# Small array tiles for the delta-rule walk of a four-mixer decoder step

## The chip, the cores and the metric

The kernel runs on one core of one Trainium2 chip. Its time is the device time of one execution in microseconds (us). Three executions of the kernel before took 2918.29, 2924.04 and 2924.26 us; the median is 2924.04 us. The engines are named as in the profile: PE (TensorE, matrix products), PEld (its weight loads), DVE (VectorE), ACT (ScalarE), POOL (GpSimd), SP (the queue that issues most transfers).

## The reference

Two layers, each `h = h + W_out @ concat(gate * mixer(RMSNorm(h)))` over 2048 prompt tokens, 16 meta tokens and 8 single decode tokens, width 1024, all float32. The four mixers (HGRN2, gated delta rule, SSD, retention) have 4 heads of 64 channels each and read columns of one input projection. The change is in the gated delta rule alone. Cut to what matters, one chunk of it is:

```python
def chunk_gated_delta(S, xs):
    q, k, v, g, beta = xs
    G = jnp.cumsum(g, axis=-1)
    m = jnp.where(strict, einsum('bhik,bhjk->bhij', k, k) * decay * beta[..., None], 0.0)
    rhs = concatenate([v * beta[..., None], k * (beta * exp(G))[..., None]], axis=-1)
    sol = triangular_solve(eye + m, rhs, lower=True, unit_diagonal=True)
    u = sol[..., :dv] - einsum('bhik,bhkv->bhiv', sol[..., dv:], S)
    qk = einsum('bhik,bhjk->bhij', q, k) * decay
    o = einsum('bhik,bhkv->bhiv', q * exp(G)[..., None], S) + einsum('bhij,bhjv->bhiv', qk, u)
    S_new = exp(g_last) * S + einsum('bhjk,bhjv->bhkv', k * exp(g_last - G)[..., None], u)
```

The outcome doesn't depend on the chunk length, and the kernel uses blocks of 32 tokens for this mixer.

## The kernel before

The tokens are cut into one short tile (t = 0: 32 prompt rows, of which 16 are meta tokens, and 8 decode rows) and 16 tiles of 128; two tiles make a dense block of 256 columns. A layer runs the SSD mixer (stage C), then the projections of the delta rule (stage B), then HGRN2 (A) and retention (D), then the output projection. The big projections multiply two-part float32r numbers in three products each (lines 473 to 475 and 483 to 485, tile `pd`). All smaller products go through the helper `mm` at line 235 in plain float32; the trace shows two PE records for each of these.

The recurrence of the delta rule, `walkB` (line 1207), is a generator. `hook` (line 145) runs its next part after each piece of dense work of stages B, A and D, so the walk's instructions lie between other matmuls on PE. A simulation-led scheduler sets the final order of instructions on each engine by when their operands would be ready. Each engine then works through its list in order.

For each tile of 128 tokens the walk does this.
- `loadB` (line 1119) issues the transfers: q, k, v (`X.qkv`) and the inverses (`X.tc`) into one buffer `bld`, the scores (`X.ma`) into `bma`. Both hold, for each token row, four heads of 32 columns: only the diagonal 32 x 32 blocks are stored.
- `keysB` (line 1138) makes the operands. POOL spreads the inverses to a matrix `tb` of 128 x 128 a head, zero outside its four diagonal blocks (line 1143). With it four products make the solved keys (`ke`, into `nq`, keys and queries of a block side by side), and four more the solved values `X.wi` (lines 1183 and 1184: `tb` against `vs`, 128 x 128 by 64 columns a head).
- `stepB` (line 1189) runs for each of the tile's four blocks. The state `SB` holds two heads a tile, block-diagonal: 128 rows (two heads of 64 channels) by 2 x 64. Two products (lines 1194 to 1196), one for each pair of heads, multiply keys and queries by the state into `X.wo`: 64 rows (32 of keys, 32 of queries) by 256 columns. DVE adds the keys' half to `wi` (line 1197), four products `kt` x `wi` make the update (line 1201; contraction over 32 rows), `next_state` (line 286) decays the state on ACT and adds the update on DVE in two halves of 64 partitions. ACT copies the queries' half to `X.oq` (line 1205).
- At the end of the tile (line 1261) four products of the scores with `wi` go into `X.wo`. For them POOL has spread the scores `X.ma` to `mb` (line 1243), 128 x 128 a head like `tb`.

Stages A and B also use parts of the array: scores of 64 rows by 32 or 64 columns (`sc<-aq,ak`, `sc<-bk`). `pair` (line 198) gives them a PSUM bank for each head half, with the note that row tiles of the array may not share a bank.

Of the kernel before, what the change touches and what calls it, by code (L numbers as in the profile page):

```python
# [92 lines left out]
def body(tc, ctx, a, o, nch, depth, blks, off):  # L93
# [39 lines left out]
    def later(f):  # L133
        """emit f after the next piece of work that is put off"""
        pend.append(f)
        while len(pend) > 1:
            pend.pop(0)()
# [7 lines left out]
    def hook(n=1):  # L145
        """the next parts of the walk that runs beside other work"""
        credit[0] += n
        while credit[0] >= 1:
            credit[0] -= 1
            if walk and next(walk[0], 0) == 0:  # L150
                walk.pop()

    @contextmanager
    def inorder(names):
        """what is emitted inside is issued after what was emitted before, on these engines"""
        seen, left = {}, set(names)
        for i in reversed(nc.cur_bb.bb.instructions):
            e = i.engine
            if e in left:
                seen[e] = i  # L160
                left.discard(e)
                if not left:
                    break
        with ExitStack() as st:
            for i in seen.values():
                st.enter_context(tc.issue_after(i))
            yield
# [31 lines left out]
    def pair():  # L199
        """a bank per head half: row tiles of the array may not share a bank"""  # L200
        return psc.tile([128, 2, 512], F32, tag="sc", name="sc")
# [43 lines left out]
    # ---------------------------------------------------------------- constants  # L245
# [15 lines left out]
    def fill():  # L261
        nc.sync.dma_start(cst, a["c_tab"])
        tri = w1([128, 128], "tri")
        nc.sync.dma_start(tri, a["c_retm"][:, 704:832])
        V.tensor_copy(l128r, tri)
        V.tensor_scalar(nbf, C("u32c"), -NEG, NEG, ALU.mult, ALU.add)
        V.tensor_copy(ibf, ident)
        tt(strict, C("u32c"), C("hm0"), ALU.subtract)
        for x in (*sbd, tb, mb, hones):
            G.memset(x, 0.0)  # L270
        G.memset(hones[0:64, 0:1], 1.0)
        G.memset(hones[64:128, 1:2], 1.0)

    # block-diagonal states (two heads a tile), in turns
# [4 lines left out]
    # full triangles (upper halves written), in turns; outside of their use: norm weights, retention's decay  # L279
# [6 lines left out]
    mb = cp.tile([128, 4, 128], F32, name="mb")  # L286

    def next_state(L, m, pu, decay):
        """S = decay * S + update, block-diagonal"""
        old = L.S[m]  # L290
        beside = m == "B"
        new = sbd[3 * beside + L.turn[beside] % (3 - beside)]
        L.turn[beside] += 1
        if old is not None:
            low = (bk if beside else w1)([128, 2, 2, 64], "low")
            for p in range(2):
                S.mul(low[:, p], old[:, p], decay(p))
        for hh in range(2):
            rr = slice(64 * hh, 64 * hh + 64)
            pv = pu[rr, 0:128].rearrange("k (p v) -> k p v", p=2)  # L300
            if old is None:
                V.tensor_copy(new[rr, :, hh], pv)
            else:
                tt(new[rr, :, hh], low[rr, :, hh], pv, ALU.add)  # L304
        L.S[m] = new
# [9 lines left out]
    # ---------------------------------------------------------------- helpers  # L315
# [4 lines left out]
    def power(dst, src, k=0):  # L320
        """src ** -0.5 (k=0) or 0.5 (k=1)"""
# [23 lines left out]
    def rms_scale(hx, R):  # L345
        """1 / rms of the rows"""
# [6 lines left out]
    # ---------------------------------------------------------------- per layer parameters  # L353
    def load_layer(l):
# [38 lines left out]
        # forget gate bounds: softmax of the logits over the depth axis, cumulative  # L393
# [34 lines left out]
    # ---------------------------------------------------------------- dense pieces  # L428
# [66 lines left out]
    def xprep(L, t, hx, keep=False):  # L495
        """normalised rows of a token tile -> channel-major, in two exact parts, to DRAM or to the block's tiles"""
# [32 lines left out]
    def rowtile(b, nm):  # L529
        """token-major rows of 256 columns by tile"""  # L530
# [6 lines left out]
    def small(L, b, raw):  # L537
        """decays and step sizes from the narrow columns of a block's tiles"""
# [31 lines left out]
        # cumulative sums: ssd over the chunk, gdn over blocks of 32  # L570
# [15 lines left out]
    def group_scale(osrc, R, groups, eps):  # L586
        """rows scaled by 1 / rms of each group, in SBUF; eps: number or [R, groups]"""
# [26 lines left out]
    def finish(t, mi, osrc, R, eps, w, z, b=None):  # L614
        """group norm of the mixer rows; returns what takes them to channel-major, gate z [128, 2, R], and to DRAM"""
# [27 lines left out]
    # decode: partitions hold (head half, key), free (sample, pair, value)  # L643
# [12 lines left out]
    def dec_bcast(rows8):  # L656
        """[8, 256] rows -> [128 (hh k), (b p), 64]"""
# [8 lines left out]
    def pb(x, cols=None):  # L666
        """[128, 2, 8] channel-major sample columns -> [128, 8, 2, 64] broadcast over values"""
# [8 lines left out]
    def dec_sum(src, lhs, m):  # L676
        """sum over the key partitions"""
# [18 lines left out]
    # ---------------------------------------------------------------- HGRN2  # L696
# [4 lines left out]
    def mixA(L, W, b):  # L701
# [26 lines left out]
        for c0, Lc, tl in groups:  # L728
# [7 lines left out]
            def scores(h, w):  # L736
                """products of keys at j and queries at j + w in steps of h"""
# [127 lines left out]
    # ---------------------------------------------------------------- short convolutions  # L865
    def conv(L, ws, b, wi, key, hasb, out):
        """out: 3 tiles [128, 2, BW] (pairs of channel tiles)"""
# [53 lines left out]
    def conv_samples(L, wi, key, hasb, src, dst):  # L921
        """the taps come from the stored rows"""
# [29 lines left out]
    # ---------------------------------------------------------------- gated delta  # L952
# [17 lines left out]
    def prepB(L, bs):  # L970
        """what the blocks need before the states: inverses of the unit triangles"""
# [4 lines left out]
        # sums of squares of q per token and head  # L976
# [30 lines left out]
        def factors(j0, j1):  # L1007
            """factors of tiles j0 .. j1 from the sums of squares of their keys"""
# [21 lines left out]
        def scv(x, n0, n):  # L1030
            """blocks n0 .. n0 + n as [(block, row), head, column]"""
            return x[:, n0:n0 + n].rearrange("h n j i -> (n j) h i")

        # decay within blocks of 32
# [13 lines left out]
        def scores(b, t, pv, start):  # L1048
            """pv [rows, x, y, p, i]: keys by keys, keys by queries"""
# [45 lines left out]
        # negated inverse of the unit triangular blocks above the diagonal: even rows of a block in one partition,  # L1095
        # odd rows in another, each beside the whole block as it was
# [23 lines left out]
    def loadB(L, P, i):  # L1120
        """what a tile keeps in DRAM: q, k, v, inverses, scores; gates"""
# [9 lines left out]
        # a group's first tile may have to wait for the inverses  # L1131
# [5 lines left out]

    def keysB(L, X):
        """a tile's operands for the walk over its blocks, in parts"""
        P, i, t, Lc = X.P, X.i, X.t, X.Lc  # L1140
        for bb in range(Lc // 32):
            r = slice(32 * bb, 32 * bb + 32)
            gtt(tb[r, :, r], X.tc[r], bcm(C("hm0")[r], 1, 4), ALU.subtract)
# [11 lines left out]
        # running decay of a block, broadcast over key channels  # L1155
# [8 lines left out]
        # keys and queries of a block side by side, in turns  # L1164
# [17 lines left out]
        for h in range(4):  # L1182
            mm(pn[0:Lc, 256 + 64 * h:320 + 64 * h], tb[0:Lc, h, 0:Lc], vs[0:Lc, h], False, True)
# [4 lines left out]
    def stepB(L, X, bb):  # L1188
        """one block of the walk"""
        r = slice(32 * bb, 32 * bb + 32)  # L1190
        SB, wt = L.S["B"], X.wi
        if SB is not None:
            b0, w0 = 64 * (bb // 2), 256 * (bb % 2)
            for p in range(2):
                mm(X.wo[b0:b0 + 64, w0 + 128 * p:w0 + 128 * p + 128], X.nq[:, p, 64 * bb:64 * bb + 64],
                   SB[:, p].rearrange("k x v -> k (x v)"), p == 0, True)
            tt(wt[r], wt[r], X.wo[r, w0:w0 + 256], ALU.add)
# [5 lines left out]
        if SB is not None:  # L1203
            o0 = 32 * (bb + 1 - 2 * (bb % 2))
            S.copy(X.oq[r], X.wo[o0:o0 + 32, w0:w0 + 256])

    def walkB(L):
        """the tiles in turn, in parts; a tile's operands are made during the one before"""
# [19 lines left out]
        while done < NT:  # L1228
# [12 lines left out]
            for bb in range(X.Lc // 32):  # L1241
                r = slice(32 * bb, 32 * bb + 32)
                gcopy(mb[r, :, r], X.ma[r])
            for bb in range(X.Lc // 32):
# [16 lines left out]
            for h in range(4):  # L1261
                mm(pi[0:X.Lc, 64 * h:64 * h + 64], mb[0:X.Lc, h, 0:X.Lc], X.wi[0:X.Lc, 64 * h:64 * h + 64], h == 0, True)
# [11 lines left out]
    def decB(L, ys, epsq):  # L1274
# [5 lines left out]
        # rows of v, keys scaled to unit length  # L1280
# [43 lines left out]
    # ---------------------------------------------------------------- SSD  # L1324
# [8 lines left out]
    def mixC(L, W, b):  # L1333
# [14 lines left out]
        def front(t):  # L1348
            """log decays of the tokens up to i, in two exact parts"""
# [88 lines left out]
    def post(L, t, osb, R):  # L1438
        """gated rows -> normalised channel-major"""
# [59 lines left out]
    # ---------------------------------------------------------------- retention  # L1499
# [3 lines left out]
    def mixD(L, W, b):  # L1503
        if b.first:
# [4 lines left out]
            # beside the triangles' use  # L1509
# [90 lines left out]
    # ---------------------------------------------------------------- output projection  # L1600
# [28 lines left out]
    # ---------------------------------------------------------------- program  # L1629
# [9 lines left out]
    def decode(L, left=False):  # L1639
        """the next part of the decode step"""  # L1640
# [113 lines left out]
def trace(nc, inputs):  # L1754
    """declares the arrays, traces the program; returns arrays by name"""
# [30 lines left out]
```

## Time and profile before

| | us |
|---|---|
| median of three executions | 2924.04 |
| profiled execution, span from first to last instruction | 2924.2 |
| PE busy | 2811.0 |
| PEld, DVE, POOL, ACT busy | 2631.0, 1694.9, 1045.4, 1010.7 |

The span of the profiled execution agrees with the median, so nothing has to be added around it. In the trace an array tile is given as rows*columns (128*64: 128 rows of contraction, 64 output partitions), then the operand as partitions x columns. A matmul record lasts longer than the time until the next one may start, since matmuls are pipelined; costs are therefore read from start to start.

### The profile page before, as it was taken

What the parts mean: (1) busy time and instruction counts of PE and PEld (TensorE: products, weight loads), DVE (VectorE), ACT (ScalarE), POOL (GpSimd) and SP (SyncE); (2) the same over time, 40 slices, a digit from 0 to 9 for tenths busy, and PEclk for the clock granted to TensorE, in tenths of its full rate; (3) what the DMA queues carried; (4) which work ended last, traced back from release to release, by engine and by line L of the source; (5) the groups of instructions that cost most, each with busy time, mean ns of one, the idle gap of its engine ahead of it and who ended that gap; (6) DMA issues with size and microseconds to landing.
All of it is one profiled execution on the core that took longest, in us unless ns stands there. A gap on an engine that the chain in (4) does not pass through costs nothing.

```text
span 2924.2 us, 76217 instructions
## 1 busy us (share of the span) xinstructions
PE 2811.0 (96%) x31196; PEld 2631.0 (90%) x31196; DVE 1694.9 (58%) x4822; ACT 1010.7 (35%) x2547; POOL 1045.4 (36%) x2000
## 2 busy tenths in 40 slices
PE   6989999999999999999999999899999999999998
PEld 6889898988888899999999999888988888999998
DVE  6777765646566745364456767565556657445433
ACT  5545522333333412232244454133333333222221
POOL 4453555665232211110033543745742222112000
PEclk9999999999999999999999999999999999999999
DMA  7243364462231432247762433645432222331433
GB/s 181 68 151 118 127 163 122 133 188 76 63 112 60 129 95 88 74 128 212 215 204 93 127 106 103 152 128 152 139 101 69 78 99 83 96 116 63 134 131 109
DMA packets 391332, 349.92 MB, mean 120 GB/s; under 512 B 144312, under 2 KB 361904, under 8 KB 380744
## 3 DMA queue, kind: packets, MB, share of 16 engines
q1 hardware_dynamic: 387464, 335.96, 37.5%
q0 software_dynamic: 3520, 9.09, 1.5%
q8 instruction: 247, 4.05, 0.6%
q14 instruction: 101, 0.83, 0.1%
HBM read 247.06 MB, written 98.10 MB: 118 GB/s over the span
## 4 chain that ended last, share of the span: by engine, by line
PE 84%; DVE 6%; DMA 4%; POOL 3%; ACT 2%; issue 2%; SPq 0%; POOLq 0%; ACTq 0%; DVEq 0%
PE pd L473 10%; PE pd L474 10%; PE pd L483 10%; PE pd L484 10%; PE pd L475 10%; PE pd L485 10%; PE tr L235 7%; PE sc L235 5%; PE wo L235 5%; PE o L235 3%; DMA wr<-in_w_in_dram 1%; PE tr L611 1%; PE tr L507 1%; DVE hx L502 1%; POOL bR L1110 1%
## 5 line engine op out<-in xcount | busy, mean ns | idle before, releaser
L473 PE MATMUL pd<-xh,wh 128*128 128x256 f32 (+1 forms) x2816 | 832.1, 296 | 12.6 <-DVE hB L901 3.3
L474 PE MATMUL pd<-xl,wh 128*128 128x256 f32 (+1 forms) x2816 | 817.9, 290 | 0.0
L475 PE MATMUL pd<-xh,wl 128*128 128x256 f32 (+1 forms) x2816 | 814.1, 289 | 0.0
L483 PE MATMUL pd<-wh,xh 128*128 128x256 f32 (+3 forms) x2448 | 702.0, 287 | 6.4 <-DVE sraw L1342 4.6
L484 PE MATMUL pd<-wl,xh 128*128 128x256 f32 (+3 forms) x2448 | 700.8, 286 | 2.5 <-POOL wl L450 2.5
L485 PE MATMUL pd<-wh,xl 128*128 128x256 f32 (+3 forms) x2448 | 698.0, 285 | 0.2
L473 PEld LDWEIGHTS pd<-xh,wh 128*128 128x128 f32 x2816 | 543.9, 193 | 37.2 <-issue 16.8
L474 PEld LDWEIGHTS pd<-xl,wh 128*128 128x128 f32 x2816 | 543.8, 193 | 9.1 <-issue 6.6
L475 PEld LDWEIGHTS pd<-xh,wl 128*128 128x128 f32 x2816 | 543.6, 193 | 4.1 <-issue 2.6
L483 PEld LDWEIGHTS pd<-wh,xh 128*128 128x128 f32 (+1 forms) x2448 | 455.7, 186 | 12.6 <-issue 5.4
L484 PEld LDWEIGHTS pd<-wl,xh 128*128 128x128 f32 (+1 forms) x2448 | 455.8, 186 | 9.0 <-issue 3.4
L485 PEld LDWEIGHTS pd<-wh,xl 128*128 128x128 f32 (+1 forms) x2448 | 455.7, 186 | 4.4 <-issue 2.1
L304 DVE TENSOR_TENSOR sbd<-low,tr 64x128 f32<-64x128 f32 x384 | 109.0, 284 | 131.8 <-PE tr L235 113.4
L600 POOL TENSOR_SCALAR fm<-fm 128x4 f32<-128x4 f32 (+3 forms) x102 | 23.7, 233 | 419.2 <-DVE fm L597 393.1
L1613 DVE TENSOR_TENSOR hx<-hx,pd 128x256 f32<-128x256 f32 (+1 forms) x136 | 57.1, 420 | 175.5 <-PE pd L485 175.2
L327 POOL TENSOR_TENSOR fm<-fm,expo 128x4 f32<-128x4 f32 (+3 forms) x136 | 129.3, 951 | 49.0 <-DVE fm L602 38.7
L331 POOL TENSOR_SCALAR rm<-rm 128x1 f32<-128x1 f32 (+1 forms) x51 | 13.7, 269 | 367.2 <-ACT junk L349 366.3
L520 ACT ACTIVATE th<-pd 128x256 f32<-128x256 f32 (+2 forms) x162 | 62.3, 384 | 231.8 <-PE pd L475 194.9
L235 PEld LDWEIGHTS sc<-aq,ak 64*32 64x32 f32 (+1 forms) x7008 | 97.0, 108 | 39.7 <-issue 16.9
L235 PE MATMUL sc<-aq,ak 64*32 64x32 f32 (+1 forms) x7008 | 129.1, 200 | 2.5 <-ACT sq L773 2.0
L1110 POOL TENSOR_TENSOR bR<-bR,bW 128x120 f32<-128x120 f32 (+14 forms) x300 | 119.6, 399 | 21.6
L1109 POOL TENSOR_TENSOR bW<-bU,bR 128x120 f32<-128x120 f32 (+14 forms) x300 | 112.6, 375 | 36.4 <-DMA bR<-bscr 15.4
(519 smaller groups left out, 4989.0 us busy)
## 6 DMA issues: line engine op xcount, KB each, us to landing
xh<-xh SPq DMA_DIRECT2D x56, 1024.0 KB
xl<-xl SPq DMA_DIRECT2D x56, 1024.0 KB
wr<-in_w_in_dram SPq DMA_DIRECT2D x64, 512.0 KB
hx<-in_x_prompt_dram SPq DMA_DIRECT2D x32, 512.0 KB
y<-y SPq DMA_DIRECT2D x128, 128.0 KB
yf<-y SPq DMA_DIRECT2D x32, 512.0 KB
bld<-qkv SPq DMA_DIRECT2D x32, 384.0 KB
xh<-xh SPq DMA_DIRECT2D x8, 1184.0 KB
```

Of the source, the lines that this page charges most:

```text
L235: T.matmul(out, l, r, start=start, stop=stop, skip_group_check=True)
L304: tt(new[rr, :, hh], low[rr, :, hh], pv, ALU.add)
L327: G.tensor_tensor(dst, src, e.broadcast_to(list(src.shape)), ALU.pow)
L473: T.matmul(ps, hi[:, d], b.xh[:, d, 0:b.n], start=(d == 0), stop=False)
L474: T.matmul(ps, hi[:, d], b.xl[:, d, 0:b.n], start=False, stop=False)
L475: T.matmul(ps, lo[:, d], b.xh[:, d, 0:b.n], start=False, stop=(d == 7))
L483: T.matmul(ps[0:R, 0:n], xh[:, d], hi, start=(d == 0), stop=False)
L484: T.matmul(ps[0:R, 0:n], xh[:, d], lo, start=False, stop=False)
L485: T.matmul(ps[0:R, 0:n], xl[:, d], hi, start=False, stop=(d == 7))
L520: act(th[0:R, 0:n], ps, AF.Tanh, scale=0.5)
L1109: f(wv, bcm(U_[0:2 * nu, j, j + 1:32], 1, m), bcl(R_[0:2 * nu, 0:m, j], 31 - j), ALU.mult)
L1110: f(R_[0:2 * nu, 0:m, j + 1:32], R_[0:2 * nu, 0:m, j + 1:32], wv, ALU.subtract)
```

## The change

The block-diagonal operands are no longer multiplied whole. The state product becomes one product for each head, 64 rows by 64 columns, on the array tile of its own head half. The two products with `tb` (values) and `mb` (scores) become one for each head and block, 32 x 32, by a new helper `blocks32`. Each reads the packed operand directly. `mb` and its copies go. `tb` stays for the product that makes `ke`; its subtraction is now done in place for the whole tile and then copied. In `X.wo` a block now has 128 columns, and the two head halves lie in the upper and lower 64 partitions; DVE's addition and ACT's copy of a block are each split in two by head half.

```diff
+    def blocks32(out, lhs, rhs, Lc, start):
+        for h in range(4):
+            for bb in range(Lc // 32):
+                r = slice(32 * bb, 32 * bb + 32)
+                mm(out(r, h), lhs[r, h], rhs[r, h], start and h == 0, True)
@@ keysB
+        gtt(X.tc[0:Lc], X.tc[0:Lc], bcm(C("hm0")[0:Lc], 1, 4), ALU.subtract)
         for bb in range(Lc // 32):
             r = slice(32 * bb, 32 * bb + 32)
-            gtt(tb[r, :, r], X.tc[r], bcm(C("hm0")[r], 1, 4), ALU.subtract)
+            gcopy(tb[r, :, r], X.tc[r])
...
-        for h in range(4):
-            mm(pn[0:Lc, 256 + 64 * h:320 + 64 * h], tb[0:Lc, h, 0:Lc], vs[0:Lc, h], False, True)
+        blocks32(lambda r, h: pn[r, 256 + 64 * h:320 + 64 * h], X.tc, vs, Lc, False)
@@ stepB
-            b0, w0 = 64 * (bb // 2), 256 * (bb % 2)
             for p in range(2):
-                mm(X.wo[b0:b0 + 64, w0 + 128 * p:w0 + 128 * p + 128], X.nq[:, p, 64 * bb:64 * bb + 64],
-                   SB[:, p].rearrange("k x v -> k (x v)"), p == 0, True)
-            tt(wt[r], wt[r], X.wo[r, w0:w0 + 256], ALU.add)
+                for hh in range(2):
+                    rr = slice(64 * hh, 64 * hh + 64)
+                    mm(X.wo[rr, 128 * bb + 64 * p:128 * bb + 64 * p + 64], X.nq[rr, p, 64 * bb:64 * bb + 64],
+                       SB[rr, p, hh], p == 0, True)
+            def part(hh, q):
+                r0 = 64 * hh + 32 * ((bb + q) % 2)
+                return X.wo[r0:r0 + 32, 128 * bb:128 * bb + 128].rearrange("t (p v) -> t p v", p=2)
+            w4 = wt.rearrange("t (p x v) -> t x p v", p=2, x=2)
+            for hh in range(2):
+                tt(w4[r, hh], w4[r, hh], part(hh, 0), ALU.add)
...
-            o0 = 32 * (bb + 1 - 2 * (bb % 2))
-            S.copy(X.oq[r], X.wo[o0:o0 + 32, w0:w0 + 256])
+            for hh in range(2):
+                S.copy(X.oq.rearrange("t (p x v) -> t x p v", p=2, x=2)[r, hh], part(hh, 1))
@@ walkB
-            for bb in range(X.Lc // 32):
-                r = slice(32 * bb, 32 * bb + 32)
-                gcopy(mb[r, :, r], X.ma[r])
...
-            for h in range(4):
-                mm(pi[0:X.Lc, 64 * h:64 * h + 64], mb[0:X.Lc, h, 0:X.Lc], X.wi[0:X.Lc, 64 * h:64 * h + 64], h == 0, True)
+            blocks32(lambda r, h: pi[r, 64 * h:64 * h + 64], X.ma, X.wi.rearrange("t (h v) -> t h v", h=4), X.Lc, True)
```

The scheduler also lays the rest out anew. On PE, one walk step in stage A of layer 0 (seventh full tile, second block; `wo<-sbd` is the state product, `pd` the dense work, `sc` HGRN2's scores) stands like this before:

```order
L484 MATMUL pd<-wl,xh 128x256
L485 MATMUL pd<-wh,xl 128x256
L235 MATMUL wo<-sbd_113,bnq 64x128 x2
L483 MATMUL pd<-wh,xh 128x256
L484 MATMUL pd<-wl,xh 128x256
```

and like this in the changed kernel (whose line numbers are one lower there):

```order
L235 MATMUL sc<-aq,ak 32x32 x20
L235 MATMUL wo<-sbd_113,bnq 64x64
L235 MATMUL sc<-aq,ak 32x32
L484 MATMUL pd<-wh,xl 128x256
L482 MATMUL pd<-wh,xh 128x256
L483 MATMUL pd<-wl,xh 128x256
L484 MATMUL pd<-wh,xl 128x256
L235 MATMUL wo<-sbd_113,bnq 64x64 x3
L482 MATMUL pd<-wh,xh 128x256
```

The four products of the step no longer stand together: the first, which needs only the first head half of the state, is put ahead of dense work, and three follow later. Over the whole program the state products of the 128 steps stand in 179 runs instead of 128, the 130 updates in 155 instead of 130, and the score products of the 34 tiles in 49 instead of 40.

On PE, between the sixth and seventh full tile (`wo<-bwi,mb` are the score products, `tr<-bvs,tb` the products with the inverses, `tr<-tb,bke` the solved keys, `tr<-bwi,bkt` the update), before:

```order
L235 MATMUL sc<-aq,ak 32x32 x14
L235 MATMUL tr<-bwi,bkt 64x64 x4
L235 MATMUL tr<-tb,bke 64x128 x4
L235 MATMUL sc<-aq,ak 32x32 x2
L235 MATMUL wo<-bwi,mb 128x64 x4
L235 MATMUL sc<-aq,ak 32x32 x11
L235 MATMUL tr<-bvs,tb 128x64 x4
L235 MATMUL sc<-aq,ak 32x32 x5
L483 MATMUL pd<-wh,xh 128x256
```

and in the changed kernel:

```order
L235 MATMUL sc<-aq,ak 32x32 x17
L235 MATMUL tr<-bwi,bkt 64x64
L235 MATMUL tr<-tb,bke 64x128 x3
L235 MATMUL tr<-bwi,bkt 64x64 x3
L235 MATMUL tr<-tb,bke 64x128
L235 MATMUL sc<-aq,ak 32x32 x6
L235 MATMUL wo<-bwi,bma 32x64 x16
L235 MATMUL sc<-aq,ak 32x32 x7
L235 MATMUL tr<-bvs,bld 32x64 x16
L235 MATMUL sc<-aq,ak 32x32 x2
L472 MATMUL pd<-xh,wh 128x256
```

Four products by head became sixteen by head and block at the same places, and the update and the solved keys are now cut into one and three. Counted over the whole order, two neighbouring matmul rows have different array tiles at 1195 places before and at 1376 in the changed kernel.

On POOL, at the same tile (`fm` are norm factors, `bgx` a broadcast of decays, `sq` HGRN2's triangles), before:

```order
L327 TENSOR_TENSOR fm<-fm,expo 128x4
L243 COPY bgx<-g 128x256
L243 COPY mb<-bma 32x4x32 x4
L1143 TENSOR_TENSOR tb<-bld,cst 32x4x32 x4
L327 TENSOR_TENSOR fm<-fm,expo 128x4
```

and in the changed kernel:

```order
L243 COPY tb<-bld 32x4x32 x4
L326 TENSOR_TENSOR fm<-fm,expo 128x4
L1147 TENSOR_TENSOR bld<-bld,cst 128x128
L243 COPY bgx<-g 128x256
L243 COPY sq_114<-aS 32x2x32 x8
```

The copies to `mb` are gone, and one subtraction on 128 partitions with four copies stands for four subtractions on 32.

## Rows read from the trace of the kernel before

**Rows 1.** The page's first part: span, engines' busy time, share, instructions.
```profile
span 2924.2 us, 76217 instructions
PE 2811.0 (96%) x31196; PEld 2631.0 (90%) x31196; DVE 1694.9 (58%) x4822; ACT 1010.7 (35%) x2547; POOL 1045.4 (36%) x2000
```
**Rows 2.** The page's chain that ended last, shares by engine.
```profile
PE 84%; DVE 6%; DMA 4%; POOL 3%; ACT 2%; issue 2%; SPq 0%; POOLq 0%; ACTq 0%; DVEq 0%
```
**Rows 3.** Waits of PE: us in total, times, longest.
```profile
PE tr L507 <- DVE hx L502: 13.2, 2, 10.4
PE tr L235 <- DVE bwi L1197: 12.3, 5, 5.3
PE tr L1146 <- DMA bld<-qkv: 11.7, 3, 6.5
```
**Rows 4.** PE groups: array tile, operand, records | busy, mean ns | idle before.
```profile
L235 PE MATMUL wo<-sbd,bnq 128*64 128x128 f32 x512 | 83.9, 287 | 0.5 <-DVE sbd L304 0.2
L235 PE MATMUL wo<-bwi,mb 128*128 128x64 f32 (+1 forms) x272 | 36.7, 274 | 0.0
L235 PE MATMUL tr<-bvs,tb 128*128 128x64 f32 (+1 forms) x272 | 34.9, 271 | 0.0
```
**Rows 5.** Timeline of PE, a state product between dense work: start us, us, what.
```profile
500.13 0.28 PE L474 MATMUL pd<-xl,wh 128*128 128x256 f32 x1
500.25 0.28 PE L475 MATMUL pd<-xh,wl 128*128 128x256 f32 x1
500.46 0.65 PE L235 MATMUL wo<-sbd,bnq 128*64 128x128 f32 x4
501.04 0.39 PE L473 MATMUL pd<-xh,wh 128*128 128x256 f32 x1
501.26 0.28 PE L474 MATMUL pd<-xl,wh 128*128 128x256 f32 x1
```
**Rows 6.** Timeline of PE, an update between dense work.
```profile
496.13 0.28 PE L473 MATMUL pd<-xh,wh 128*128 128x256 f32 x1
496.33 0.45 PE L235 MATMUL tr<-bwi,bkt 32*64 32x64 f32 x8
496.71 0.39 PE L474 MATMUL pd<-xl,wh 128*128 128x256 f32 x1
496.94 0.28 PE L475 MATMUL pd<-xh,wl 128*128 128x256 f32 x1
```
**Rows 7.** Timeline of PE, HGRN2's 64-wide scores around an update.
```profile
794.32 0.45 PE L235 MATMUL sc<-aq,ak 64*64 64x64 f32 x8
794.70 0.45 PE L235 MATMUL tr<-bwi,bkt 32*64 32x64 f32 x8
795.07 0.45 PE L235 MATMUL sc<-aq,ak 64*64 64x64 f32 x8
```
**Rows 8.** Timeline of PE, the products with the inverses between small scores.
```profile
721.42 1.10 PE L235 MATMUL tr<-bvs,tb 128*128 128x64 f32 x8
722.46 0.32 PE L235 MATMUL sc<-aq,ak 64*32 64x32 f32 x10
```
**Rows 9.** Timeline of PE, the score products of tile 0 (one block).
```profile
462.49 0.63 PE L235 MATMUL wo<-bwi,mb 32*32 32x64 f32 x8
463.05 1.02 PE L235 MATMUL tr<-dV,hones 128*2 128x512 f32 x2
```
**Rows 10.** Timeline of PE, a long run of small scores.
```profile
682.45 0.82 PE L235 MATMUL sc<-aq,ak 64*32 64x32 f32 x64
683.20 0.38 PE L474 MATMUL pd<-xl,wh 128*128 128x256 f32 x1
```
**Rows 11.** DVE and ACT groups by shape: as rows 4.
```profile
L1197 DVE TENSOR_TENSOR bwi<-bwi,wo 32x256 f32<-32x256 f32 x128 | 53.3, 416 | 82.9 <-PE wo L235 81.0 <-PE o L235 0.4
L1067 DVE TENSOR_TENSOR bma<-sc,bdc 32x128 f32<-32x128 f32 x2 | 0.6, 278 | 0.1
```
**Rows 12.** Waits of POOL, columns as rows 3.
```profile
POOL mb L243 <- PE wo L235: 151.7, 23, 12.7
```
**Rows 13.** Waits of SP, columns as rows 3.
```profile
SPq L1130 <- DVE bnq L1169: 83.6, 10, 12.1
```

More of the change, by code (lines that the diff above doesn't have):

```diff
@@ L268, in fill @@
         tt(strict, C("u32c"), C("hm0"), ALU.subtract)
-        for x in (*sbd, tb, mb, hones):
+        for x in (*sbd, tb, hones):
             G.memset(x, 0.0)
@@ L285, in body @@
     tb = cp.tile([128, 4, 128], F32, name="tb")
-    mb = cp.tile([128, 4, 128], F32, name="mb")
     def next_state(L, m, pu, decay):
```

## The prediction

> **What bounds the kernel now.** I read the page's first part, then the chain, the waits of PE and, for prices, the timeline of PE. The first part shows PE busy for 2811.0 of 2924.2 us, while DVE, ACT and POOL are far below [rows 1]. The chain that ended last is PE for 84% [rows 2]: the reader is to see that the span is one long queue of matmuls. PE's waits are short. The three longest together are 37.2 us, and of these only the second and third have to do with the walk (24.0 us) [rows 3]. So what changes the length of PE's list changes the time nearly one for one, and what changes DVE, ACT or POOL counts only where PE comes to wait for it.
>
> The groups that the change touches are 512 + 272 + 272 records of PE [rows 4]. Their busy figures overlap, as a record lasts longer than the distance to the next, so I price everything from start to start.
>
> **Prices.** Dense matmuls follow each other at 0.12 us (500.13 to 500.25) [rows 5]. A state product, four records of 128 columns in one array tile, takes 0.58 us until dense work starts again [rows 5]. An update, eight records of 64 columns, takes 0.38 [rows 6]; HGRN2's 64 x 64 scores, also eight of 64 columns, take 0.38 too [rows 7]. In both of these two array tiles work side by side (the update's are two column halves, the scores' two row halves), so eight records are four steps. Four steps of 128 columns against four of 64 differ by 0.20 us, so a step of 64 columns is 0.05, and 0.18 of the 0.38 is fixed. The fixed part is the price of changing the array's tile. Rows 6 give the same: from 496.13 to 496.94 are 0.81 us, less 0.24 for two dense distances and 0.20 for four steps leaves 0.37 for two changes. Rows 7, where small tiles follow small tiles, give 0.375 - 0.20, about 0.17. One array tile alone checks the step: tile 0's score products, eight records of 64 columns in a single 32 x 32 tile, take 0.56, which is 8 x 0.05 + 0.16 [rows 9]. I use 0.16 to 0.185 for a change, and 0.16 in the sum, since most of the added ones stand beside small groups.
>
> **The change part by part.**
>
> State products. 128 steps each exchange four records of 128 columns (0.58) for eight of 64 columns in two tiles, upper rows to upper partitions and lower to lower. The 64 x 64 scores are the nearest row: 0.38. That is -0.20 x 128 = -25.6 us. If the two tiles took turns it would be 8 x 0.05 + 0.18 = 0.58, a gain of nothing.
>
> Products by block. 32 tiles, two groups each, make 64 visits. Before, eight records on the full array take 1.04 us between small scores (721.42 to 722.46) [rows 8]: the same 64 columns cost twice as much there as in a small tile. After, a visit has 32 records: four array tiles on the diagonal, eight records each. No row shows four diagonal tiles. From below, if records only had to be issued, the long run of small scores gives 64 records in 0.75 us, so 32 cost 0.37 [rows 10], which lies under the tile's own eight steps; so the best case is 8 x 0.05 + 0.18 = 0.58. From above, if the tiles take turns, 32 x 0.05 + 0.18 = 1.78. I take 0.58, because two column tiles in one bank [rows 6] and two row tiles in two banks [rows 7] both run side by side, and diagonal tiles share neither rows nor output partitions. That is -0.46 x 64 = -29.4 us; the bounds are -29 and +47.
>
> Changes of tile. The order shows 181 more places where neighbouring rows differ in array tile. They come from steps that the scheduler now cuts (51 more runs of state products, 25 of updates, 9 of score products) and from visits that stood in full-array surroundings. 181 x 0.16 = +29.0 us (33.5 at 0.185).
>
> Other engines. DVE's addition becomes two of 32 x 128: 2 x 278 - 416 = +0.14 us a step [rows 11], ACT's copy grows likewise, +18 us at most over 128 steps if all of it were in PE's way. It isn't: PE waited for this addition in only 5 steps [rows 3], because a step's update follows its state product by several us of dense work (496.33 after the one before, 500.46 the next [rows 5, 6]). I cost it at nothing; without that cover it is 18 us. POOL loses the copies to `mb`, before which it sat idle for 151.7 us [rows 12], which frees whatever stood behind them; no wait of PE's three longest ends there, so nothing too. The buffer `bld` is now held until the products with the inverses, later than its last reader before (`bnq`), for which SP already waits 10 times [rows 13]. PE waited for that load in 3 tiles [rows 3]; if each of these waited another 7 us, roughly the distance of two steps, it is 21 us. I take nothing, as the load is issued a tile ahead.
>
> Sum: -25.6 - 29.4 + 29.0 = -26.0. From the profiled span of 2924.2, which is the median of the runs within 0.2, that is 2898 us.
>
> **A rule against it.** What the trace shows is side-by-side work for row tiles only with a bank for each [rows 7], and the kernel's own `pair` is written for that. The Trainium skill, TensorEngine Tiling (Array Packing), Restrictions and Gotchas, says that different row tiles cannot access the same PSUM bank at once. The changed kernel does let them: four row tiles write one bank of `pn` or `wo`, each to its own partitions. No run here shows whether distinct partitions lift the rule; by it the sum would be that of the first rival, by the rows it stays.
>
> **Rivals.**
>
> First, slower: row tiles that write one bank take turns. Place: the 64 visits and the 128 state products. Price: (1.78 - 1.04) x 64 = +47.4, state products 0, changes +29.0, together +76, so 3000 us (2985 to 3025). For it speaks `pair`'s note and that no row shows the case; against it that column tiles do share a bank [rows 6]. It decides below two tiles at a time: with two, a visit is 16 x 0.05 + 0.18 = 0.98, which gains 4 us in all.
>
> Second, no change: exactly that case, two at a time in the 32 x 32 groups. -25.6 - 4 + 29 = -0.6, so 2924.
>
> Third, the work shrinks and PE waits instead: the longer step on DVE and ACT (up to 18) and the later release of `bld` (up to 21) come out, with the split steps making each half of a state product wait for its half of the state. 2898 + 39 = 2937 at worst, about 2918 if half comes. For it: 24.0 us of such waits exist now [rows 3]. Against: they come in 8 places out of 128 steps.
>
> **How the numbers follow.** Forecast 0.60, with its own range 2882 to 2914 (the price of a change, some waits more or fewer). First rival 0.16, second 0.10, third 0.14. A measurement of this kernel can tell 0.2% (6 us) from no change. Faster by more than that is the forecast and a third of the third rival: 0.64. Within: the second and about a third of the third, 0.14. Slower: the first, and the rest, 0.22. The range 2880 to 2955 holds forecast, second and third; it leaves out the first (0.16) and a little below.
>
> **What would show it.** PE's records should rise by 2 x (2 x 32 x 12 + 128 x 2) = 2048 to about 33244. A run of 8 state records should take 0.38 to the next start, a visit of 32 records 0.55 to 0.65; 1.8 says the first rival, 1.0 the second. Updates in two runs with 0.16 to 0.18 lost at each edge confirm the third term. PE's waits for `bwi` and `bld` well above 24 us would be the third rival. The prediction is wrong if the visits come out at the size of rows 8 or more, or if PE's waits grow by more than the 26 us saved.

## The result, and the profile after

The changed kernel takes 2889.51 us (median of 4 executions, 2883.72 to 2890.53), against 2924.15 us of the kernel before beside it: a ratio of 0.9885, 95% interval 0.9865 to 0.9906. That is 34.6 us less; 26 were forecast. The profiled execution went from a span of 2924.2 to 2887.0 us, 37.2 us less.

The first part of the profile's page, which answers to [rows 1], and its chain by engine, which answers to [rows 2]:

```profile
span 2887.0 us, 80538 instructions
PE 2788.1 (97%) x33244; PEld 2605.7 (90%) x33244; DVE 1717.3 (59%) x4950; ACT 1030.2 (36%) x2675; POOL 997.6 (35%) x1903
...
PE 82%; DVE 6%; POOL 3%; DMA 3%; ACT 2%; issue 2%; SPq 1%; POOLq 0%; ACTq 0%; DVEq 0%
```

PE has the 2048 more records that were counted, and is busy for 22.9 us less. It still bounds the kernel. The waits of PE, in us, times and longest, as [rows 3]:

```profile
PE tr L506 <- DVE hx L501: 13.0, 2, 10.3
PE sc L235 <- POOL cgu L1364: 10.7, 6, 4.4
...
PE pd L472 <- ACT bk L896: 5.6, 4, 1.7
PE tr L235 <- POOL tb L243: 5.1, 1, 5.1
...
PE tr L235 <- DVE bwi L1212: 1.7, 2, 1.3
PE tr L1153 <- DMA bld<-qkv: 1.7, 1, 1.7
```

The two waits that had to do with the walk (`bwi` 12.3 and `bld` 11.7 us before) are down to 1.7 each, where the third rival had them grow.

The products with the inverses between dense work, on PE's timeline (start us, us, what); [rows 8] showed them before, between small scores:

```profile
475.88 0.28 PE L474 MATMUL pd<-xh,wl 128*128 128x256 f32 x1
476.09 0.65 PE L235 MATMUL tr<-bvs,bld 32*32 32x64 f32 x32
476.67 0.39 PE L472 MATMUL pd<-xh,wh 128*128 128x256 f32 x1
476.89 0.28 PE L473 MATMUL pd<-xl,wh 128*128 128x256 f32 x1
```

32 records take 0.58 us from start to start, as forecast: four diagonal tiles that write one bank work side by side. Within the visit the trace starts four records within 0.02 us, and each next four 0.06 to 0.08 us later. A state product in one piece, which answers to [rows 5]:

```profile
479.48 0.28 PE L474 MATMUL pd<-xh,wl 128*128 128x256 f32 x1
479.69 0.45 PE L235 MATMUL wo<-sbd,bnq 64*64 64x64 f32 x8
480.07 0.39 PE L472 MATMUL pd<-xh,wh 128*128 128x256 f32 x1
480.29 0.28 PE L473 MATMUL pd<-xl,wh 128*128 128x256 f32 x1
```

0.38 us, again as forecast. And one that the scheduler has cut:

```profile
837.23 0.28 PE L474 MATMUL pd<-xh,wl 128*128 128x256 f32 x1
837.44 0.33 PE L235 MATMUL wo<-sbd,bnq 64*64 64x64 f32 x2
837.69 0.39 PE L472 MATMUL pd<-xh,wh 128*128 128x256 f32 x1
837.92 0.28 PE L473 MATMUL pd<-xl,wh 128*128 128x256 f32 x1
838.13 0.44 PE L235 MATMUL wo<-sbd,bnq 64*64 64x64 f32 x6
838.50 0.39 PE L474 MATMUL pd<-xh,wl 128*128 128x256 f32 x1
838.72 0.28 PE L472 MATMUL pd<-xh,wh 128*128 128x256 f32 x1
```

The single product takes 0.25 us and the other three 0.37, together 0.62 for 0.38 in one piece. The reader is to see why: alone in its tile, the first product's two records have nobody beside them, and of the three others one tile has four records and the other two. Six steps stand for four, besides the second entry and exit. The whole price of the cut is read from dense record to dense record: 837.23 to 838.72 are 1.49 us, less four dense distances of 0.12 leaves 1.01; in one piece 479.48 to 480.29 are 0.81, less two leaves 0.57. So this cut costs 0.44 us.

**Where the time went, by a count over the trace.** For every pair of neighbouring PE records I took the distance of their starts and subtracted the median distance of the same pair (tile, columns, operands, with or without a change just before) in all traces of this study. An excess over 0.3 us counts as a wait; the excess of over 20 ns at records in stretches whose granted clock is half (1.2 GHz) counts as clock; the rest is PE's work. Each column is from one profiled execution; the ends of the span (about 18 us) are left out. Cuts are runs of state products above 128, plus runs of updates above 130; changes are places in PE's order where the array tile differs, all relative to the kernel before.

| kernel | median us | ratio and 95% interval | changes | cuts | span | work | waits | clock |
|---|---|---|---|---|---|---|---|---|
| before | 2924.15 | | 0 | 0 | 2924.2 | 2785.0 | 86.6 | 34.3 |
| changed | 2889.51 | 0.9885 (0.9865 to 0.9906) | +181 | 76 | 2887.0 | 2763.1 | 73.3 | 32.4 |
| e1 state products only | 2925.59 | 1.0027 (1.0015 to 1.0039) | +114 | 68 | 2922.9 | 2784.8 | 85.6 | 34.7 |
| e2 products by block only | 2886.68 | 0.9888 (0.9870 to 0.9905) | +25 | 0 | 2895.1 | 2758.2 | 84.5 | 34.6 |
| e3 tile by tile | 2940.80 | 1.0076 (1.0058 to 1.0093) | +169 | 81 | 2940.6 | 2809.0 | 77.0 | 36.7 |
| e4 late half first | 2885.10 | 0.9879 (0.9858 to 0.9900) | +70 | 16 | 2871.4 | 2738.0 | 85.7 | 29.4 |
| e5 changed, longer step | 2922.35 | 1.0007 (0.9993 to 1.0022) | +111 | 49 | 2921.7 | 2751.0 | 92.0 | 59.5 |
| e6 as e1, late half first | 2901.02 | 0.9939 (0.9919 to 0.9960) | -10 | 8 | 2901.7 | 2760.4 | 81.5 | 41.4 |
| e7 as e4, own buffer | 2881.10 | 0.9866 (0.9850 to 0.9883) | +58 | 13 | 2879.8 | 2735.4 | 94.1 | 32.2 |
| e8 before, split adds | 2906.89 | 0.9964 (0.9951 to 0.9978) | +18 | 1 | 2904.3 | 2791.6 | 74.8 | 19.7 |
| e9 before, longer step | 2918.18 | 0.9994 (0.9982 to 1.0005) | -42 | 2 | 2915.7 | 2785.3 | 79.4 | 32.8 |
| e10 changed again | 2887.61 | 0.9880 (0.9859 to 0.9901) | +181 | 76 | 2886.5 | 2762.6 | 74.5 | 31.0 |
| e11 as e7, again | 2878.55 | 0.9856 (0.9837 to 0.9875) | +58 | 13 | 2876.0 | 2735.3 | 94.3 | 28.0 |
| e12 as e2, split adds | 2900.56 | 0.9947 (0.9928 to 0.9966) | +18 | 1 | 2895.3 | 2758.9 | 88.9 | 29.4 |

Of the 37.2 us, 21.9 are less work of PE, 13.3 are shorter waits, 1.9 are clock. The line between work and waits hangs on how the pairs are formed: by shape alone, or by all operand names, the work of the changed kernel comes out 17 to 28 us less and its waits 18 to 7 us less, while the clock stays within 1 to 2. So differences of up to some 5 us in these two columns prove nothing.

### The profile page after: what moved, and what is told of

It is laid out like the page before. It is cut to its first block, busy times and chain, and to the rows that moved or that the text cites. A ratio compares the mean times of both kernels' runs of the same rounds, so it can differ in the third digit from the quotient of the medians.

```text
span 2887.0 us, 80538 instructions
## 1 busy us (share of the span) xinstructions
PE 2788.1 (97%) x33244; PEld 2605.7 (90%) x33244; DVE 1717.3 (59%) x4950; ACT 1030.2 (36%) x2675; POOL 997.6 (35%) x1903
## 4 chain that ended last, share of the span: by engine, by line
PE 82%; DVE 6%; POOL 3%; DMA 3%; ACT 2%; issue 2%; SPq 1%; POOLq 0%; ACTq 0%; DVEq 0%
PE pd L482 10%; PE pd L483 10%; PE pd L484 10%; PE pd L472 10%; PE pd L474 10%; PE pd L473 9%; PE tr L235 7%; PE sc L235 5%; PE wo L235 4%; PE o L235 3%; PE tr L610 1%; PE tr L506 1%; POOL bW L1108 1%; DMA wr<-in_w_in_dram 1%; POOL bR L1109 1%
## 5 line engine op out<-in xcount | busy, mean ns | idle before, releaser
L472 PEld LDWEIGHTS pd<-xh,wh 128*128 128x128 f32 x2816 | 541.1, 192 | 41.9 <-issue 12.1
```

The costliest lines, as they stand in the source:

```text
L472: T.matmul(ps, hi[:, d], b.xh[:, d, 0:b.n], start=(d == 0), stop=False)
```

## The experiments

Ratios are to the kernel before, run beside each group on the same chip (2916.37 to 2919.64 us there).

**Which half of the change carries it: e1 and e2.** e1 takes the changed kernel and puts `tb` and `mb` back for values and scores:

```diff
-        blocks32(lambda r, h: pn[r, 256 + 64 * h:320 + 64 * h], X.tc, vs, Lc, False)
+        for h in range(4):
+            mm(pn[0:Lc, 256 + 64 * h:320 + 64 * h], tb[0:Lc, h, 0:Lc], vs[0:Lc, h], False, True)
```

> State products on 64 x 64 tiles as in the changed kernel; the products by block back on the full array with tb and mb. Theory (time is the work of PE plus the changes of array tile): state products -25.6 us, and the order has 114 more changes than before at 0.16 = +18, so 2924 - 7 = 2917 us (2908 to 2922). Rival (the gain came from POOL no longer waiting to fill mb, and from PE's shorter waits): this keeps mb, so 2924 or a little more, and the products by block would carry all of the 34 us.

Measured: 2925.59 us, slower by 0.27% (0.15 to 0.39), outside the theory's range and at the rival's number. The work of PE is 2784.8 against 2785.0 us: nothing is left of 25.6, where 7 were to be left.

e2 takes the changed kernel and puts the state product, its addition and its copy back:

```diff
-                    mm(X.wo[rr, 128 * bb + 64 * p:128 * bb + 64 * p + 64], X.nq[rr, p, 64 * bb:64 * bb + 64],
-                       SB[rr, p, hh], p == 0, True)
+                mm(X.wo[b0:b0 + 64, w0 + 128 * p:w0 + 128 * p + 128], X.nq[:, p, 64 * bb:64 * bb + 64],
+                   SB[:, p].rearrange("k x v -> k (x v)"), p == 0, True)
```

> Products by block on 32 x 32 tiles as in the changed kernel; state products back on 128 x 64. Theory: -29.4 us for 64 visits, 25 more changes of tile than before at 0.16 = +4, so 2924 - 25 = 2899 us (2890 to 2906), visits of 0.58 us in the trace. Rival (POOL's share): about 2890, the changed kernel's whole gain without the state products.

Measured: 2886.68 us, as fast as the whole change and below the theory's range. Its work is 26.8 us less, where 25.4 were expected; the median fell by some 33, so the number is at the rival's, but the waits of its trace (84.5) are near those of before, and the work is there. Its profiled execution was its slowest (2896.83) and had a granted clock of 0.984, the other four 0.987 to 0.990; part of their gain is not in the trace. By their times alone e1 and e2 both speak for the rival. Against it speaks e6 below, which keeps `mb` and its copies and is still 18 us faster than the kernel before.

**Whether four tiles work side by side by themselves: e3.** The loops of `blocks32` are exchanged.

```diff
-        for h in range(4):
-            for bb in range(Lc // 32):
+        for bb in range(Lc // 32):
+            for h in range(4):
```

> The changed kernel with the loops of blocks32 exchanged: all four heads of one 32 x 32 tile follow each other, then the next tile. Same products. Theory (a tile works beside another only if PE's queue has reached the other's products, and it holds back behind one busy tile): a visit goes from 0.58 towards 32 x 0.05 + 0.18 = 1.78 us, 64 x 1.2 = up to +75 us, 2930 to 2965. Rival (the queue looks ahead over all 32 records): a visit stays at 0.58 to 0.65, 2890 to 2895.

Measured: 2940.80 us, slower than before. The timeline of PE in e3:

```profile
472.77 0.28 PE L474 MATMUL pd<-xh,wl 128*128 128x256 f32 x1
472.98 1.39 PE L235 MATMUL tr<-bvs,bld 32*32 32x64 f32 x32
474.30 0.39 PE L472 MATMUL pd<-xh,wh 128*128 128x256 f32 x1
```

The same 32 records take 1.32 us instead of 0.58, and 0.74 x 64 = 47 us is what the work column shows (2809.0 - 2763.1 = 45.9). The same products on the same tiles gain or lose by the order in which they are issued. In this visit the first five records start one by one, 0.05 to 0.08 us apart, and only from there on do some lie side by side.

**What a cut costs: e4 and e6.** The head halves are taken in the order 1, 0, so that a step's first product needs the half of the state that is written last, and all four become ready together.

```diff
-                for hh in range(2):
+                for hh in (1, 0):
                     rr = slice(64 * hh, 64 * hh + 64)
...
-        for h in range(4):
+        for h in (1, 0, 3, 2):
```

> The changed kernel with the head halves of the state product and of the update in the order 1, 0: the first product of a step needs the half that is written last, so the scheduler keeps the four together (144 runs of state products for 179, 130 of updates for 155, 111 fewer changes of tile in the order). Theory (a change costs 0.16 us of PE): 2889 - 18 = 2872 us (2866 to 2879). Rival (the changes are free, since PE waits a little anyway, or the early first product saves as much in waits): 2886 to 2893.

Measured: 2885.10 us, between the two ranges, and no clear difference from the changed kernel's 0.9885. The work fell by 25.1 us more than in the changed kernel, more than the 18 expected, but the waits rose by 12.4. Its executions range from 2873.14 us (the profiled one, clock 0.985) to 2891.74 (the other four have 0.981 to 0.984), so at the median more came back than the trace shows.

e6 makes the same edit in e1:

> State products alone on 64 x 64 tiles as in e1, but with the head halves in the order 1, 0 in state product and update, so that the four products of a step stay together (136 runs instead of 170, updates 130 instead of 156, 10 fewer changes of tile than in the kernel before). Theory (the state products' own gain of 0.20 us a step is real and e1 lost it to cut groups: two more changes and two more steps of a single tile for each cut): 2919.5 - 26 = 2894 us (2888 to 2901). Rival (64 x 64 tiles save nothing in this program, whatever the order): 2916 to 2926, as e1.

Measured: 2901.02 us, ratio 0.9939, clearly faster than e1. Work fell by 24.6 us (26.4 by the sum). So the state products' own gain is real when a step stays in one piece, and e1 lost it to its 68 cuts. 7 us of clock took part of it back.

**Whether the longer step is covered: e5 and e9.** Between state product and update, the block's values are multiplied by 1.0.

```diff
             for hh in range(2):
                 tt(w4[r, hh], w4[r, hh], part(hh, 0), ALU.add)
+            V.tensor_scalar(wt[r], wt[r], 1.0, None, ALU.mult)
```

> The changed kernel with one more DVE operation in every step: after the two additions the block's 32 x 256 values are multiplied by 1.0 in place, between state product and update. The order has 70 fewer changes of array tile, since the update now waits for one writer and is no longer cut (130 runs instead of 155). Theory (PE's list sets the time, a step's DVE work is covered, and 25 cuts fewer save 0.3 to 0.4 us each): 2878 to 2888 us. Rival (the walk's chain of DVE and ACT is in PE's way): at least 0.2 us more in each of 128 steps, 2889 + 25 = 2915 or more.

Measured: 2922.35 us, the rival's number: 33 us more than the changed kernel. Its work is 12.1 us less, as the fewer cuts and changes say, but waits are 18.7 and clock 27.1 us more. The largest wait of PE in e5 is for the added operation itself (line 1213); in the changed kernel PE waited 1.7 us for the block's values:

```profile
PE tr L235 <- DVE bwi L1213: 14.5, 11, 3.1
```

The mean granted clock of the changed kernel and of e5:

```profile
core 0: 2887.0 us, clock 0.985
```
```profile
core 0: 2921.7 us, clock 0.974
```

and PE in e5 at one place, where PE sat idle for 0.85 us and shortly before for 1.69 us, and then by stretches (start and end, length, busy time and instructions of PE, PEld, DVE, ACT and POOL, granted clock, DMA share and GB/s), first over 30 us and then in parts:

```profile
693.34 0.54 PE L235 MATMUL sc<-aq,ak 64*32 64x32 f32 x38 [1.69 <-issue]
...
699.01 0.68 PE L235 MATMUL sc<-aq,ak 64*64 64x64 f32 x16 [0.85 <-ACT sq L772]
699.87 0.45 PE L235 MATMUL tr<-bwi,bkt 32*64 32x64 f32 x8 [0.18 <-DVE bwi L1213]
```
```profile
690.00:720.00 30.00, 27.28 (x402) 24.37 (x400) 15.14 (x50) 9.49 (x30) 12.22 (x39) 0.72 0.30 74
...
691.00:693.50 2.50, 0.81 (x55) 0.56 (x59) 0.00 (x0) 0.00 (x0) 1.87 (x6) 1.00 1.14 260
693.50:697.20 3.70, 3.70 (x59) 3.50 (x50) 2.51 (x9) 0.69 (x2) 2.19 (x11) 0.54 0.40 63
697.20:700.00 2.80, 1.77 (x62) 1.35 (x62) 2.05 (x8) 1.80 (x7) 2.38 (x11) 1.00 0.13 47
700.00:710.00 10.00, 10.00 (x119) 8.72 (x118) 6.13 (x20) 3.60 (x12) 3.81 (x8) 0.53 0.31 68
```

A clock of 0.72 over 30 us is a bit more than half of the stretch at 1.2 GHz. In the parts, each of the two stretches in which PE was partly idle ran at the full clock, and the one behind it at little more than half. The same 30 us of the changed kernel's trace have 0.83. A theory that the walk's chain is in PE's way was the natural reading, and e9 tests it with the same operation in the kernel before.

> The kernel before with the extra DVE operation of e5 (0.30 us in each of 128 steps) and nothing else; 42 fewer changes of tile in its order. If a longer step costs PE waits and clock in any arrangement: e5's loss of about 35 to 45 us again, less 42 x 0.16 = 7, so 2945 to 2957. If e5's loss was an accident of one order of instructions: 2910 to 2920.

Measured: 2918.18 us, no difference (0.9994, 0.9982 to 1.0005), although the added operation takes 0.32 us there and PE still waits for `bwi`:

```profile
L1198 DVE TENSOR_SCALAR bwi<-bwi 32x256 f32<-32x256 f32 x128 | 40.9, 319 | 3.6
```
```profile
PE tr L235 <- DVE bwi L1198: 12.2, 8, 4.1
```

So 41 us more of DVE work in the steps cost nothing there: in the kernel before the step is covered, and a longer step doesn't cost PE in every arrangement. In e5 the edit also made another order, and 12.8 of its 18.7 us more waits are for the added operation; whether the order or the operation lost them, no run separates.

**The split additions alone: e8 and e12.** In the kernel before, the addition and the copy are cut in two by columns, in the addition the first columns last, so that PE's products stay as they are.

```diff
-            tt(wt[r], wt[r], X.wo[r, w0:w0 + 256], ALU.add)
+            for c in (128, 0):
+                tt(wt[r, c:c + 128], wt[r, c:c + 128], X.wo[r, w0 + c:w0 + c + 128], ALU.add)
```

> The kernel before, with DVE's addition and ACT's copy of each step cut in two by columns (two of 32 x 128 each, as many as in the changed kernel); products and array tiles as before, no step cut on PE (129 runs of state products, 130 of updates, 18 more changes of tile). Theory of the prediction (the longer step is covered): 18 x 0.16 = +3, 2919 to 2926. Rival (the step is in PE's way, as e5 says): +0.14 us of DVE in 128 steps, 18 us and more with the clock: 2935 to 2945.

Measured: 2906.89 us, faster than before by 0.36% (0.22 to 0.49), which neither theory expected. PE's work rose by 6.6 us; waits fell by 11.8 and clock by 14.6. The twelve executions have a median granted clock of 0.9885, the kernel before beside them 0.985. e12 makes the same edit in e2, to see whether these gains belong to the edit:

> e2 (products by block on 32 x 32 tiles, state products as before) with the additions and copies of a step cut in two as in e8. If cutting them is itself worth 12 us, because each half comes out earlier, the gains add: 2919.6 - 33 - 13 = 2874 us (2870 to 2880). If e8's 12 us were an accident of one order of instructions (PE's waits and the clock after them): anything from 2875 to 2895, with the work of PE at full clock as in e2.

Measured: 2900.56 us, 15.8 less than before and slower than either range, while e2 had 33 less. The same edit took 12.7 us off one kernel and put about 17 on another, with PE's work within 1 us of e2's. The two profiled executions don't show the 17, their spans are 2895.3 and 2895.1 us; but over all executions the median granted clock is 0.983 in e12 and 0.988 in e2, worth at most some 14 us of 2890 (an estimate from these shares). So the edit has no worth of its own that carries over. That the order which comes with it decides is the nearest reading, not shown by a run.

**A version that beats both: e7, e10, e11.** e7 is e4 with a buffer of its own for the inverses:

```diff
-        X.tc = raw[:, 768:896].rearrange("j (h i) -> j h i", h=4)
+        X.tc = k2.tile([128, 4, 32], F32, tag="btc", bufs=2, name="btc")
```

> e4 (halves in the order 1, 0) with the inverses in a buffer of their own of two, so that the buffer of q, k, v is free again once keys and queries are made, as in the kernel before. Theory (the later release of that buffer costs PE little): as e4, 2880 to 2888. Rival (e4's runs lie up to 14 us above its profiled one because PE waits for that load): 2868 to 2876, with the wait for bld below 3 us.

Measured: 2881.10 us, in the theory's range. PE still waits for the load of q, k and v (7.9 us, once, against 12.5 in e4), so the early release doesn't take this wait away, and the rival's number isn't reached. For a comparison on one chip the changed kernel (e10) and e7 (e11) ran together.

> The changed kernel itself, beside e11 on the same chip. Both theories: 2885 to 2890 us.

> e7 again, beside e10 on the same chip. Theory (fewer cuts on PE, 0.2 us each for a change and its lost side-by-side steps): 5 to 10 us below e10. Rival (the shorter list on PE is given back in waits): within 4 us of e10.

Measured: 2887.61 (2880.63 to 2890.92) and 2878.55 us (2876.04 to 2879.92). No execution of e11 is as slow as the fastest of e10, a difference of 9 us. PE's work is 27.3 us less, and waits are 19.8 us more: some seven tenths of the shorter list were given back.

## Why the prediction was right, point by point

The direction and the shorter list of PE came as forecast. That the time came out beyond the forecast is luck: the list alone gave about 22 us of the 26, and 13 us of shorter waits, for which the sum had nothing and whose cause is open, came on top.

- State products: right in size. 0.38 us for a step in one piece, and e6, which has few cuts, measures 24.6 us of work for them.
- Products by block: right. Visits of 0.58 us; e2 measures 26.8 us of work for -29.4 + 4.
- Changes of tile: the term that was mis-sized. "181 x 0.16 = +29.0 us" priced a cut as two changes, 0.32 us; the timelines above give 0.44. The difference is about the two steps, 0.10 us, that no longer lie side by side with others. With 0.10 for each cut added, the sum gives for PE's work -0.6 in e1 (-25.6 + 114 x 0.16 + 68 x 0.10; measured -0.2, without the cuts -7.4), -26.4 in e6 (measured -24.6), -42 in e4 (-47.0), -44 in e7 and e11 (-49.6, -49.7) and -18 in the changed kernel (-21.9). Only in e1 do the cuts improve the fit clearly; in the others the sum misses by 2 to 5 us with them or without, which is no more than the count can tell. So the state products, half of the forecast gain, brought nothing in e1 because changes and cuts together ate about as much (18 and 7 us).
- Other engines at nothing: e9 bears out for the kernel before that a longer step is covered. The prediction's two times for this cover are those of an update (496.33) and of the next state product (500.46); what counts is the way from a state product to its own update. In the trace of the kernel before, the state product of that update stands 3.4 us ahead of it (start us, us, what):

```profile
492.96 0.65 PE L235 MATMUL wo<-sbd,bnq 128*64 128x128 f32 x4
```

  So the reading holds. But the forecast had no term for the order. The waits fell by 13.3 us in the changed kernel and again in e10 (12.1), and this is most of what brought the gain from about 22 to 37 us in the profile. The waits for `bwi` and `bld` fell by 20.6 us there, and others rose. The cause was not isolated: e2 has no `mb` and waits only 2.1 us shorter, so leaving out POOL's copies doesn't do it alone, and e8 has waits as much shorter with `mb` and the old products. Orders that differ by a few instructions had waits of 73 to 94 us and 20 to 60 us of clock.
- First rival: wrong. Four tiles that write one bank, each to its own partitions, run side by side (0.58 us for 32 records, 1.78 forecast for taking turns); e3, with the same tiles and the same bank, loses by the order of issue. The rule of the Trainium skill, TensorEngine Tiling (Array Packing), Restrictions and Gotchas, that row tiles cannot access one bank at once, is not borne out by these 0.58 us, where their output partitions differ.
- Second and third rival: wrong; a visit is 0.58, not 0.98, and the two waits named there fell from 24.0 to 3.4 us. What the third describes is seen in e5, where waits and clock ate more than the shorter list gave.

## What to carry to other kernels

Where PE's list is the bound, cutting a block-diagonal product into small array tiles pays about by the steps that then run side by side, if neighbouring instructions alternate between tiles (0.58 against 1.32 us here); count the changes of array tile (about 0.16 us each here, and 0.44 for a step cut in two) in the final order, not in the code. Keep a group of small products whole: let the first of them need the operand that is written last. With a scheduler that lays out the whole program anew, an edit worth nothing can move the time by about 0.5% through waits and the clock (e8, e12), so an edit's own worth is read from PE's work in the trace and not from one timing.

## What was not expected of the hardware

PE reaches the next array tile late: in e3, with eight records of a tile in a row, 32 records took 1.32 us, a good deal below the 1.78 estimated for tiles that take turns and far above 0.58. And idle time on PE was followed by stretches at 1.2 GHz that cost more than the idle time: at the place shown, 1.69 us and then 1.03 us of idle PE stood before stretches with a granted clock of 0.54 and 0.53. In all, e5 has 18.7 us more waits and 27.1 us more at the lower clock; that the waits caused all of the latter is not shown.
